# S5 mixer: part of u scaled through a diagonal, first two gelus alone, six tiles of the gated GEMM in split parts

## The chip, the cores and the metric

The program runs on one core of one Trainium2 chip. The metric is the device time of one execution in microseconds, as the median of several runs. TensorE (PE), its weight loads (PEld), VectorE (DVE), ScalarE (ACT), GpSimd (POOL) and the DMA queue of SyncE (SP) each run their own list of instructions in the order written and wait for one another by semaphores. TensorE's clock has two levels, 1.2 and 2.4 GHz; the profile shows the granted one as a share of 2.4 GHz.

## The reference

Two layers over x of 256 rows (sequence) by 2048 columns, in float32. Layer 0 is a differential attention, layer 1 the S5 mixer; each is followed by a squared-relu MLP, with an rmsnorm ahead of each of the four and at the end. The change touches the S5 mixer alone:

```python
h = rmsnorm(x, norm_mix[1])                 # x * rstd(row) * gain
u = h.reshape(B, S, 128 groups, 16)
bu = B_bar u ; x_t = a x_(t-1) + bu_t       # complex diagonal state, per group
y = Re(C x) + d_skip * h
g = gelu(y)
val, gate = split(g @ w_glu, 2)             # w_glu is 2048 x 4096
x = x + val * sigmoid(gate)
```

## The kernel before

x stays in SBUF as two row tiles `xres[0]`, `xres[1]` of 128 x 2048. Weights come from HBM in chunks of two 128-row k-tiles by 512 columns (512 KB, tag `raw`, 5 buffers). `prep` (L181) cuts a chunk into two fp32r parts: ACT writes the high part `wh` (L191) and DVE the rest `wl` (`sub`, L113), four buffers each. Every GEMM outside the S5 phase takes three matmuls per product, high by high, high by low, low by high (`ktile`, L199, lines L201 to L203), from a left side that is split in the same way.

The S5 phase (`s5_phase`, L1092) handles the 2048 columns as 16 tiles of 128. For tile j:

- `s5_u` (L999) transposes x of two tiles on TensorE into one PSUM bank (L1004), and ACT copies the bank out in 16 pieces (L1009) in another order. The tiles 0 to 7 are done before the phase; the tiles 8 to 15 in the loop, at the end of the steps 1, 3, 5 and 7.
- `s5_scale` (L1013) multiplies u of two tiles by rstd in the permuted order (`rsb`). `rsb` comes from a small matmul into the bank `prs` (L1100) and a copy (L1102). The first pair is scaled on DVE, the others on POOL.
- `s5_e` (L1019): 32 matmuls into an `sd` bank (L1026), then on DVE two products, add, subtract, two scans, two products and a subtract, and one add on POOL (L1047). The result X[j] is the state that enters `s5_y`.
- `s5_y` (L1050): 48 matmuls (L1061) into a `y` bank that two tiles share. After the second tile ACT does gelu in 16 pieces (L1068), then casts g to the high part `blk.h` of the left side for the later GEMMs (L1072), and POOL subtracts to get the low part `blk.l` (L1073).
- `glu_tile` (L1079): the first 512 value and 512 gate columns of the GEMM, four float32 matmuls of 512 columns (L1085) from g and the raw weight chunk, without a split. It runs three steps behind (`LAG`).

The order in the loop is written out by hand. Step j issues `s5_e(j+1)`, the scale of tile j+4, `glu_tile(j-3)`, `s5_y(j)`, `s5_u(j+7)` at odd j, and the table fetch of tile j+4 on SP (`s5_fetch`, L978: three DMAs of 512 KB). After the loop the three last `glu_tile` follow. There are eight PSUM banks: four accumulators, two `sd` banks in turn (4 and 5), two `y` banks in turn (6 and 7). `s5_u` takes an `sd` bank too:

```python
rings["sd"], rings["y"] = [4, 5], [6, 7]
groups = [(0, 1), (2, 3), (4, 5), (6, 7), (8, 9), (10, 11), (12, 13), (14,), (15,)]
```

`keep_warm` (L320) issues matmuls whose results nobody reads: 18, 4 and 12 of them (`WARM`) while the head of the phase waits. After the phase `evict_val` (L1262) and `evict_gate` (L1270) empty the accumulators, and the next GEMMs take `glu_lhs`.

Of the kernel before, what the change touches and what calls it, by code (L numbers as in the profile page):

```python
# [16 lines left out]
P = 128  # L17
# [5 lines left out]
KB = 4  # L23
# [15 lines left out]
Q = 4  # L39

SLOTS_HOP = 3
WARM = (18, 4, 12)
LAG = 3


class Lhs:
# [11 lines left out]
def tile_trunk(  # L58
# [39 lines left out]
    def bank():  # L98
        return ring("sd")

    def tmp(shape, tag, bufs=None, dt=F32):
        if bufs is None:
            return sb.tile(shape, dt, tag=tag, name=nm(tag))
        return sb.tile(shape, dt, tag=tag, name=nm(tag), bufs=bufs)
# [10 lines left out]
    def tsc(o, a, s1, op0, s2=None, op1=None):  # L115
        if op1 is None:
            v.tensor_scalar(out=o, in0=a, scalar1=s1, scalar2=None, op0=op0)
        else:
            v.tensor_scalar(out=o, in0=a, scalar1=s1, scalar2=s2, op0=op0, op1=op1)
# [21 lines left out]
    def until(cond):  # L141
        while not cond():
            assert side
            pump()
# [32 lines left out]
    def load_next():  # L177

        load(len(raws))

    def prep(i):  # L181
        if i >= len(stream) or i in preps or GLU0 <= i < GLU0 + 16:
            return
        r = raws[i]
        h = wp.tile([P, WK, BW], F32R, tag="wh", name=nm("wh"), bufs=LIVE)
        l = wp.tile([P, WK, BW], F32R, tag="wl", name=nm("wl"), bufs=LIVE)
        preps[i] = (h, l)
        step = 1 if i < FINE else WK
        for k in range(0, WK, step):
            sl = slice(k, k + step)  # L190
            act.copy(h[:, sl], r[:, sl])  # L191
            if FINE <= i < POOL:
                sub(l[:, 0], r[:, 0], h[:, 0].bitcast(F32))
                pool_e.tensor_tensor(out=l[:, 1], in0=r[:, 1], in1=h[:, 1].bitcast(F32), op=ALU.subtract)
            else:
                sub(l[:, sl], r[:, sl], h[:, sl].bitcast(F32))
        load_next()

    def ktile(accs, lhs, k, wh, wl, t, first, last):  # L199
        ts = slice(t * P, (t + 1) * P)  # L200
        pe.matmul(accs[t], lhs.h[:, k, ts], wh, start=first, stop=False)  # L201
        pe.matmul(accs[t], lhs.h[:, k, ts], wl, start=False, stop=False)  # L202
        pe.matmul(accs[t], lhs.l[:, k, ts], wh, start=False, stop=last)  # L203
# [20 lines left out]
    def new_accs():  # L224
        return [ring("acc") for _ in range(NT)]
# [94 lines left out]
    def keep_warm(n):  # L320

        if n == 0:
            return
        a = ring("acc")
        for _ in range(n):
            pe.matmul(a, x1[3].h[:, 0, 0:P], x1[3].h[:, 0:2], start=True, stop=True)
# [669 lines left out]
        pool_e.memset(dk[:, :, 0:1], 0.0)  # L996
        return dk

    def s5_u(j):  # L999

        ps = bank().rearrange("p (i s) -> p i s", s=S)
        for i in range(2):
            for t in range(NT):
                pe.transpose(ps[:, i, t * P:(t + 1) * P], xres[t][:, (j + i) * P:(j + i + 1) * P], ident)  # L1004
        u = tmp([P, 2, Q, NCH], "vsb", bufs=4)
        pv = ps.rearrange("p i (k s) -> p i s k", s=L)
        for s in range(L):
            for q in range(Q):
                act.copy(u[32 * s:32 * s + 32, :, q], pv[32 * q:32 * q + 32, :, L - 1 - s])  # L1009
            yield s  # L1010
        U[j] = u

    def s5_scale(j, rsb, eng=pool_e):  # L1013
        u = U[j]
        uv = u.rearrange("p i q k -> p (i q) k")
        eng.tensor_tensor(out=uv, in0=uv, in1=rsb[:, None, :].broadcast_to([P, 2 * Q, NCH]), op=ALU.mult)
        U[j], U[j + 1] = u[:, 0], u[:, 1]

    def s5_e(j):  # L1019
        te, to, tt, ct = tab[j]  # L1020
        u, dk = U[j], DK.pop(j)
        pe_ = bank().rearrange("p (i q k) -> p i q k", i=2, q=Q)
        for i in range(2):
            for q in range(Q):
                for h in (slice(0, GP), slice(GP, P)):
                    pe.matmul(pe_[h, i, q], te[:, i, q, h], u[:, q], start=True, stop=True)  # L1026
        sh = [P, 2, Q, NCH]
        tw = tmp([P, 2] + sh[1:], "c5")
        t1, t2 = tw[:, 0], tw[:, 1]
        mult(t1, pe_, ct[:, 0:1].broadcast_to(sh))  # L1030
        mult(t2, pe_, ct[:, 1:2].broadcast_to(sh))
        add(t1[:, 0], t1[:, 0], t2[:, 1])
        sub(t1[:, 1], t1[:, 1], t2[:, 0])
        zz = tmp(sh, "s2k", bufs=7)
        for i in range(2):
            v.tensor_tensor_scan(out=zz[:, i].rearrange("p q k -> p (q k)"), data0=dk.rearrange("p q k -> p (q k)"),
                                 data1=t1[:, i].rearrange("p q k -> p (q k)"), initial=0.0,
                                 op0=ALU.mult, op1=ALU.add)
        n = NCH - 1
        shn = [P, 2, Q, n]  # L1040
        w1, w2 = tmp(sh, "s2k", bufs=7), tmp(sh, "s2k", bufs=7)
        mult(w1[:, :, :, 0:n], zz[:, :, :, 0:n], ct[:, 0:1, :, 0:n].broadcast_to(shn))
        mult(w2[:, :, :, 0:n], zz[:, :, :, 0:n], ct[:, 1:2, :, 0:n].broadcast_to(shn))
        xp = tmp(sh, "bc", bufs=4)
        pool_e.memset(xp[:, :, :, 0:1], 0.0)
        sub(xp[:, 0, :, 1:], w1[:, 0, :, 0:n], w2[:, 1, :, 0:n])
        pool_e.tensor_tensor(out=xp[:, 1, :, 1:], in0=w1[:, 1, :, 0:n], in1=w2[:, 0, :, 0:n], op=ALU.add)  # L1047
        X[j] = xp

    def s5_y(grp):  # L1050
# [25 lines left out]
        for jj, j in enumerate(grp):  # L1076
            G[j] = g[:, jj]

    def glu_tile(j):  # L1079

        g = G.pop(j)
        c, kk = GLU0 + j // WK * 2, j % WK
        for i, accs in ((c, a_v), (c + 1, a_g)):
            for t in range(NT):
                pe.matmul(accs[t], g[:, t * P:(t + 1) * P], raws[i][:, kk], start=j == 0, stop=j == NJ - 1)  # L1085
            if j == NJ - 1 and i == c:
                first_vals.extend(evict_val(a_v))
            if kk == WK - 1:
                load_next()
                pos[0] += 1  # L1090

    def s5_phase(norm):  # L1092
        until(lambda: norm.done)
        keep_warm(WARM[0])
        ar = tmp([P, NT, P], "s1k", bufs=4)
        for t in range(NT):
            tsc(ar[:, t], sela.rearrange("p s r -> p (s r)"), norm.rstd[:, t:t + 1], ALU.mult)
        prs = bank()[:, 0:NCH]
        for t in range(NT):
            pe.matmul(prs, ar[:, t], selb[:, t], start=(t == 0), stop=(t == NT - 1))  # L1100
        rsb = tmp([P, NCH], "rsb", bufs=1)
        v.tensor_copy(rsb, prs)  # L1102
        keep_warm(WARM[1])
        s5_scale(0, rsb, v)
        for j in range(3):
            DK[j] = s5_dk(j)
        s5_scale(2, rsb)
        s5_e(0)
        keep_warm(WARM[2])
        groups = [(0, 1), (2, 3), (4, 5), (6, 7), (8, 9), (10, 11), (12, 13), (14,), (15,)]  # L1110
        ys = {}
        for grp in groups:
            gen = s5_y(grp)
            for j in grp:
                ys[j] = (gen, j == grp[-1])
        for j in range(NJ):
            if j + 1 < NJ:
                s5_e(j + 1)
            if j + 3 < NJ:
                DK[j + 3] = s5_dk(j + 3)  # L1120
            if j % 2 == 0 and j + 4 < NJ and j + 4 in U:
                s5_scale(j + 4, rsb)
            if j >= LAG:
                glu_tile(j - LAG)
            gen, end = ys[j]
            next(gen)
            if end:
                for _ in gen:
                    pass
            if j % 2 == 1 and j + 7 < NJ:  # L1130
                for _ in s5_u(j + 7):
                    pass
            s5_fetch(j + 4)
            pump()
        for j in range(NJ - LAG, NJ):
            prep(GLU0 + 16 + j - NJ + LAG)
            glu_tile(j)


    x0 = [Lhs() for _ in range(NB)]  # L1140
# [121 lines left out]
    def evict_val(accs):  # L1262
        vs = []
        for t in range(NT):
            n = tmp([P, BW], "vsb", bufs=4)
            act.copy(n, accs[t])
            vs.append(n)
        return vs

    def evict_gate(accs, vs, u):  # L1270
        for t in range(NT):
            sg = tmp([P, BW], "s2k", bufs=7)
            act.activation(sg, accs[t], AF.Sigmoid)  # L1273
            mult(vs[t], vs[t], sg)
            xs = xres[t][:, u * BW:(u + 1) * BW]
            add(xs, xs, vs[t])
        spawn(xT_block(x3[u], u, 2, norm3, "a"), 2)

    a_v, a_g = new_accs(), new_accs()
    s5_phase(norm2)  # L1280
    evict_gate(a_g, first_vals, 0)
    for u in range(1, NB):
        a = gemm(glu_lhs)
        vs = evict_val(a)
# [60 lines left out]
```

## Time and profile before

| | |
|---|---|
| median of 3 runs | 2136.08 us (2135.87 to 2137.46) |
| profiled execution | 2133.82 us, its span 2132.0 us |
| PE busy | 2082.6 us (98%) |
| PEld, DVE, ACT, POOL busy | 1765.5, 1365.7, 1050.6, 164.6 us |
| granted clock, mean | 0.992 |
| S5 phase in the span | about 1130 to 1281 us |

The busy shares are means over the whole program. TensorE sets the time nearly everywhere; in the slices of the span one place stands out, where PE falls to 7 tenths, PEld to 4 and the clock below 9: the S5 phase. All times below are microseconds from the start of the span.

### The profile page before, as it was taken

To read this page: it belongs to the slowest core of one execution; us is meant where nothing else is said; L and a number is where in the kernel's file an instruction comes from. 1 tells how busy PE (TensorE), PEld (TensorE's weight loads), DVE (VectorE), ACT (ScalarE), POOL (GpSimd) and SP (SyncE) were. 2 spreads that over 40 slices of the span, in tenths; PEclk is the share of its full clock that TensorE was granted. 3 is DMA by queue.
4 is the path that set the end of the run, shared out by engine and by line. 5 is a ranking of instruction groups with operands and counts; after the bars stand their busy time and mean duration, and the time that the engine had idled before them with its cause. 6 is when DMAs were issued, how large, how long until landed. Compare 5 with 4: busy or idle time off the path is not lost. (4 is left out here: it accounts for less than half of the span.)

```text
span 2132.0 us, 31756 instructions
## 1 busy us (share of the span) xinstructions
PE 2082.6 (98%) x12098; PEld 1765.5 (83%) x12098; DVE 1365.7 (64%) x2284; ACT 1050.6 (49%) x1598; POOL 164.6 (8%) x282
## 2 busy tenths in 40 slices
PE   8999999999999999999997799999999999999998
PEld 8899988888888888888885457888888888888886
DVE  5775656788588667767766465556555645655655
ACT  5445545555445545544483565545434434434443
POOL 2000200021021002101102220000000000000000
PEclk9999999999999999999999899999999999999999
DMA  7467755687676867876785656565556556555553
GB/s 247 157 198 233 248 179 173 222 246 268 230 235 212 295 215 224 281 237 222 238 288 206 234 181 205 181 217 176 203 193 189 189 193 193 174 207 188 193 192 129
DMA packets 230813, 452.57 MB, mean 212 GB/s; under 512 B 20818, under 2 KB 29348, under 8 KB 230660
## 3 DMA queue, kind: packets, MB, share of 16 engines
q1 hardware_dynamic: 218400, 416.34, 58.9%
q0 software_dynamic: 11440, 32.86, 4.8%
q8 instruction: 95, 1.56, 0.3%
q10 hardware_dynamic: 820, 1.34, 0.2%
q14 instruction: 58, 0.48, 0.1%
HBM read 420.85 MB, written 41.68 MB: 217 GB/s over the span
## 5 line engine op out<-in xcount | busy, mean ns | idle before, releaser
L113 DVE TENSOR_TENSOR wl<-raw,wh 128x1024 fp32r<-128x1024 f32 (+1 forms) x690 | 833.5, 1218 | 581.7 <-ACT wh L191 577.7
L191 ACT CAST wh<-raw 128x1024 fp32r<-128x1024 f32 (+1 forms) x690 | 713.0, 1047 | 633.1 <-PE acc L203 344.9
L201 PE MATMUL acc<-wh,x 128*128 128x512 f32 x832 | 326.5, 392 | 2.4 <-ACT s2k L1273 2.4
L203 PE MATMUL acc<-wh,x 128*128 128x512 f32 x832 | 324.0, 389 | 0.0
L202 PE MATMUL acc<-wl,x 128*128 128x512 f32 x832 | 323.9, 389 | 0.0
L265 PE MATMUL acc<-x,wh 128*128 128x512 f32 x1024 | 273.9, 394 | 2.8 <-DVE s2k L110 2.8
L265 PE MATMUL acc<-a,wh 128*128 128x512 f32 x1024 | 272.7, 393 | 0.0
L201 PE MATMUL acc<-wh,a 128*128 128x512 f32 x640 | 251.6, 393 | 0.0
L202 PE MATMUL acc<-wl,a 128*128 128x512 f32 x640 | 249.4, 390 | 0.1
L203 PE MATMUL acc<-wh,a 128*128 128x512 f32 x640 | 249.3, 390 | 0.0
L265 PEld LDWEIGHTS acc<-x,wh 128*128 128x128 f32 x1024 | 177.2, 189 | 29.0 <-DVE s2k L110 3.2
L265 PEld LDWEIGHTS acc<-a,wh 128*128 128x128 f32 x1024 | 177.4, 189 | 25.0
L201 PEld LDWEIGHTS acc<-wh,x 128*128 128x128 f32 x832 | 156.2, 188 | 34.8 <-ACT s2k L1273 3.3
L203 PEld LDWEIGHTS acc<-wh,x 128*128 128x128 f32 x832 | 156.2, 188 | 32.9
L202 PEld LDWEIGHTS acc<-wl,x 128*128 128x128 f32 x832 | 156.3, 188 | 31.9
L269 PEld LDWEIGHTS acc<-a,wl 128*128 128x128 f32 x1024 | 152.8, 190 | 18.7
L269 PEld LDWEIGHTS acc<-x,wl 128*128 128x128 f32 x1024 | 152.4, 190 | 18.8
L269 PE MATMUL acc<-x,wl 128*128 128x256 f32 x1024 | 158.0, 282 | 0.0
L269 PE MATMUL acc<-a,wl 128*128 128x256 f32 x1024 | 157.5, 281 | 0.0
L248 PE MATMUL acc<-x,wh 128*128 128x256 f32 x512 | 148.5, 290 | 1.2 <-ACT wh L191 1.2
L250 PE MATMUL acc<-x,wl 128*128 128x256 f32 x512 | 145.7, 284 | 0.0
L249 PE MATMUL acc<-x,wh 128*128 128x256 f32 x512 | 145.5, 284 | 0.0
(238 smaller groups left out, 2140.8 us busy)
## 6 DMA issues: line engine op xcount, KB each, us to landing
raw<-in_mlp_w_dram SPq DMA_DIRECT2D x512, 512.0 KB
raw<-in_a_w_in_dram SPq DMA_DIRECT2D x94, 512.0 KB
raw<-in_b_w_glu_dram SPq DMA_DIRECT2D x64, 512.0 KB
raw<-in_a_w_out_dram SPq DMA_DIRECT2D x32, 512.0 KB
scr<-t POOLq DMA_DIRECT2D x32, 512.0 KB, 5.4
teo<-scr SPq DMA_DIRECT2D x32, 512.0 KB
t<-scr SPq DMA_DIRECT2D x16, 512.0 KB
pwr<-pwn SPq DMA_DIRECT2D x16, 256.0 KB
```

What stands on the lines that cost most here:

```text
L113: v.tensor_tensor(out=o, in0=a, in1=b, op=ALU.subtract)
L191: act.copy(h[:, sl], r[:, sl])
L201: pe.matmul(accs[t], lhs.h[:, k, ts], wh, start=first, stop=False)
L202: pe.matmul(accs[t], lhs.h[:, k, ts], wl, start=False, stop=False)
L203: pe.matmul(accs[t], lhs.l[:, k, ts], wh, start=False, stop=last)
L248: pe.matmul(o, wh[:, kk, cs], lhs.h[:, k], start=f and c % 2 == 0, stop=False)
L249: pe.matmul(o, wh[:, kk, cs], lhs.l[:, k], start=False, stop=False)
L250: pe.matmul(o, wl[:, kk, cs], lhs.h[:, k], start=False, stop=e and c % 2 == 1)
L265: pe.matmul(a[c], wh, lhs.hl[:, k].rearrange("p i s -> p (i s)"), start=first, stop=False)
L269: pe.matmul(a[c][:, S:], wl, lhs.h[:, k], start=False, stop=last)
```

## The change

- `s5_u` can take a diagonal matrix `diag` (rstd of the row on its diagonal) in place of the identity. The transposes of tiles 8 to 15 become ordinary float32 matmuls of x by `diag`, and their u comes out scaled: the POOL multiplications for the pairs 8, 10, 12 and 14 go. ACT makes `diag` in two activations.
- u of the tiles 8 to 11 is done before the loop, after `s5_e(0)`; u of 12 and 13 at the end of step 2, of 14 and 15 at the end of step 4. The third `keep_warm` has 4 matmuls in place of 12. The new u tiles lie in other buffers (one `wh` buffer, the tags `ct` and `junk`).
- The first pair is scaled by DVE straight from the bank `prs`; the copy `rsb` comes after.
- One gelu on a single element is issued at the head of the phase.
- The tiles 0 and 1 have gelus of their own. `glu_tile(0)` moves to step 2, `glu_tile(1)` to step 3, step 4 has none, and from step 5 on the lag is three as before.
- For the tiles 8 to 13 the weight chunks go through `prep`, two at each of the steps 9, 11 and 13, and `glu_tile` takes `ktile` with `blk.h` and `blk.l`: twelve fp32r matmuls in place of four float32 ones. `prep` issues the next weight load itself.

```diff
-WARM = (18, 4, 12)
+WARM = (18, 4, 4)
 LAG = 3
+WHOLE = 8
     def prep(i):
-        if i >= len(stream) or i in preps or GLU0 <= i < GLU0 + 16:
+        if i >= len(stream) or i in preps or GLU0 <= i < GLU0 + 16 and not WHOLE <= (i - GLU0) // 2 * WK < NJ - 2:
             return
-    def s5_u(j):
+    def s5_u(j, u=None, diag=None):
...
-                pe.transpose(ps[:, i, t * P:(t + 1) * P], xres[t][:, (j + i) * P:(j + i + 1) * P], ident)
-        u = tmp([P, 2, Q, NCH], "vsb", bufs=4)
+                o, xs = ps[:, i, t * P:(t + 1) * P], xres[t][:, (j + i) * P:(j + i + 1) * P]
+                if diag is None:
+                    pe.transpose(o, xs, ident)
+                else:
+                    pe.matmul(o, xs, diag[:, t], start=True, stop=True)
...
     def glu_tile(j):
...
-        for i, accs in ((c, a_v), (c + 1, a_g)):
+        for i, accs in ((c, A["v"]), (c + 1, A["g"])):
             for t in range(NT):
-                pe.matmul(accs[t], g[:, t * P:(t + 1) * P], raws[i][:, kk], start=j == 0, stop=j == NJ - 1)
+                if i in preps:
+                    wh, wl = preps[i]
+                    ktile(accs, blk, j % KB, wh[:, kk], wl[:, kk], t, j == 0, j == NJ - 1)
+                else:
+                    pe.matmul(accs[t], g[:, t * P:(t + 1) * P], raws[i][:, kk], start=j == 0, stop=j == NJ - 1)
...
             if kk == WK - 1:
-                load_next()
+                if i in preps:
+                    del preps[i]
+                else:
+                    load_next()
                 pos[0] += 1
     def s5_phase(norm):
         until(lambda: norm.done)
+        act.activation(warm_act, warm_act, AF.Gelu_apprx_tanh)
         keep_warm(WARM[0])
         ar = tmp([P, NT, P], "s1k", bufs=4)
+        diag = wp.tile([P, NT, P], F32, tag="wl", name="diag", bufs=LIVE)
         for t in range(NT):
             tsc(ar[:, t], sela.rearrange("p s r -> p (s r)"), norm.rstd[:, t:t + 1], ALU.mult)
+            act.activation(diag[:, t], ident, AF.Copy, scale=norm.rstd[:, t:t + 1])
...
+        keep_warm(WARM[1])
+        s5_scale(0, prs, v)
         v.tensor_copy(rsb, prs)
-        keep_warm(WARM[1])
-        s5_scale(0, rsb, v)
...
         s5_e(0)
+        u8 = wp.tile([P, 2, 2, Q, NCH], F32, tag="wh", name="u8", bufs=LIVE)
+        for i in range(2):
+            for _ in s5_u(8 + 2 * i, u8[:, i], diag):
+                pass
         keep_warm(WARM[2])
+        A["v"], A["g"] = new_accs(), new_accs()
-        groups = [(0, 1), (2, 3), (4, 5), (6, 7), (8, 9), (10, 11), (12, 13), (14,), (15,)]
+        groups = [(0,), (1,), (2, 3), (4, 5), (6, 7), (8, 9), (10, 11), (12, 13), (14,), (15,)]
...
-            if j % 2 == 0 and j + 4 < NJ and j + 4 in U:
+            if j in (0, 2):
                 s5_scale(j + 4, rsb)
-            if j >= LAG:
-                glu_tile(j - LAG)
+            if j % 2 == 1 and WHOLE <= j - 1 and j + 1 <= NJ - 2:
+                for i in range(2):
+                    prep(GLU0 + j - 1 + i)
+            if j in (2, 3) or j >= 2 + LAG:
+                glu_tile(glu)
+                glu += 1
...
-            if j % 2 == 1 and j + 7 < NJ:
-                for _ in s5_u(j + 7):
+            if j in (2, 4):
+                u = tmp([P, 2, Q, NCH], "ct" if j == 2 else "junk", bufs=1)
+                for _ in s5_u(12 if j == 2 else 14, u, diag):
                     pass
```

## Rows read from the trace of the kernel before

**Rows 1.** Waits of PE, 1125 to 1285: us in total, times, longest.

```profile
PE sd L1026 <- ACT vsb L1009: 21.4, 4, 7.0
PE y L1061 <- issue: 5.2, 3, 2.2
...
PE acc L1085 <- ACT s2k L1068: 0.6, 1, 0.6
```

**Rows 2.** Timeline around the second stall: start, duration, engine, line; idle before in brackets.

```profile
1171.00 6.58 ACT L1068 ACTIVATE s2k<-y 32x128 f32<-32x128 f32 x16 [8.37 <-PE y L1061]
...
1177.61 0.62 ACT L1072 CAST x<-s2k 128x512 fp32r<-128x512 f32 x1
...
1178.26 4.28 ACT L1009 COPY vsb<-sd 32x128 f32<-32x128 f32 x16
...
1182.59 1.97 PE L1026 MATMUL sd<-vsb,teo 128*64 128x64 f32 x32 [4.79 <-ACT vsb L1009]
```

**Rows 3.** Chain that ended last: the last stall's step, and an unstalled step.

```profile
1223.18 1.97 PE sd L1026 x32
1225.15 5.22 PE acc L1085 x8
1230.37 1.55 PE y L1061 x48
1231.92 0.93 PE sd L1026 x32
1232.85 3.63 PE acc L1085 x8
```

**Rows 4.** Windows: stretch, length, busy PE, PEld, DVE, ACT, POOL; clock, DMA, GB/s.

```profile
1150.00:1160.00 10.00, 3.31 (x84) 2.75 (x82) 8.45 (x16) 9.69 (x25) 3.16 (x8) 1.00 0.64 218
1160.00:1170.00 10.00, 7.32 (x62) 4.39 (x64) 4.93 (x9) 2.52 (x10) 2.81 (x6) 0.66 0.00 0
...
1181.00:1184.00 3.00, 1.41 (x26) 1.41 (x28) 0.00 (x0) 1.48 (x6) 1.06 (x2) 0.50 0.96 389
```

**Rows 5.** Timeline of the phase's head.

```profile
1134.90 0.66 PE L1100 MATMUL sd<-selb,s1k 128*128 128x64 f32 x4
...
1135.60 0.23 DVE L1102 COPY rsb<-sd 128x64 f32<-128x64 f32 x1 [0.56 <-PE sd L1100]
1135.86 0.69 DVE L1016 TENSOR_TENSOR vsb<-vsb,rsb 128x512 f32<-128x512 f32 x1
...
1137.80 1.29 DVE L107 TENSOR_TENSOR c<-sd,t 128x512 f32<-128x512 f32 x2 [1.25 <-PE sd L1026]
...
1149.88 1.28 ACT L1068 ACT_TABLE_LOAD   x1 [17.40 <-PE y L1061]
```

**Rows 6.** Timeline of the phase's end.

```profile
1263.70 4.64 ACT L1068 ACTIVATE s2k<-y 32x64 f32<-32x64 f32 x16
...
1268.26 10.57 PE L1085 MATMUL acc<-raw,s2k 128*128 128x512 f32 x24
...
1281.25 0.50 PE L201 MATMUL acc<-wh,x 128*128 128x512 f32 x1 [2.42 <-ACT s2k L1273]
```

**Rows 7.** Timeline of TensorE in a GEMM with split parts, before the phase.

```profile
1107.82 0.39 PE L202 MATMUL acc<-wl,a 128*128 128x512 f32 x1
...
1108.05 0.39 PE L203 MATMUL acc<-wh,a 128*128 128x512 f32 x1
```

**Rows 8.** The page's costliest groups: busy, mean ns of one, idle before.

```profile
L113 DVE TENSOR_TENSOR wl<-raw,wh 128x1024 fp32r<-128x1024 f32 (+1 forms) x690 | 833.5, 1218 | 581.7 <-ACT wh L191 577.7
L191 ACT CAST wh<-raw 128x1024 fp32r<-128x1024 f32 (+1 forms) x690 | 713.0, 1047 | 633.1 <-PE acc L203 344.9
```

**Rows 9.** Timeline: the four transposes of one u, and POOL's low part of a pair.

```profile
1170.88 0.66 PE L1004 MATMUL sd<-ident,xres 128*128 128x128 f32 x4
...
1178.31 1.26 POOL L1073 TENSOR_TENSOR x<-s2k,x 128x512 fp32r<-128x512 f32 x1 [7.48 <-ACT x L1072]
```

**Rows 10.** Windows, columns as in rows 4: a stretch with many transfers.

```profile
1193.00:1196.00 3.00, 3.00 (x8) 1.18 (x7) 2.97 (x6) 2.92 (x8) 0.00 (x0) 1.00 0.98 396
```

More of the change, by code (lines that the diff above doesn't have):

```diff
@@ L1003, in s5_u @@
             for t in range(NT):
-                pe.transpose(ps[:, i, t * P:(t + 1) * P], xres[t][:, (j + i) * P:(j + i + 1) * P], ident)
-        u = tmp([P, 2, Q, NCH], "vsb", bufs=4)
+                o, xs = ps[:, i, t * P:(t + 1) * P], xres[t][:, (j + i) * P:(j + i + 1) * P]
[3 more added lines that the diff above has]
+                    pe.matmul(o, xs, diag[:, t], start=True, stop=True)
+        if u is None:
+            u = tmp([P, 2, Q, NCH], "vsb", bufs=4)
         pv = ps.rearrange("p i (k s) -> p i s k", s=L)
@@ L1010, in s5_u, with s5_scale @@
             yield s
-        U[j] = u
-    def s5_scale(j, rsb, eng=pool_e):
+        if diag is None:
+            U[j] = u
+        else:
+            U[j], U[j + 1] = u[:, 0], u[:, 1]
+    def s5_scale(j, factor, eng=pool_e):
         u = U[j]
         uv = u.rearrange("p i q k -> p (i q) k")
-        eng.tensor_tensor(out=uv, in0=uv, in1=rsb[:, None, :].broadcast_to([P, 2 * Q, NCH]), op=ALU.mult)
+        eng.tensor_tensor(out=uv, in0=uv, in1=factor[:, None, :].broadcast_to([P, 2 * Q, NCH]), op=ALU.mult)
         U[j], U[j + 1] = u[:, 0], u[:, 1]
@@ L1077, in s5_y @@
             G[j] = g[:, jj]
+    A = {}
     def glu_tile(j):
-        g = G.pop(j)
+        g, blk = G.pop(j), glu_lhs[j // KB]
         c, kk = GLU0 + j // WK * 2, j % WK
-        for i, accs in ((c, a_v), (c + 1, a_g)):
+        for i, accs in ((c, A["v"]), (c + 1, A["g"])):
             for t in range(NT):
-                pe.matmul(accs[t], g[:, t * P:(t + 1) * P], raws[i][:, kk], start=j == 0, stop=j == NJ - 1)
+                if i in preps:
[3 more added lines that the diff above has]
+                    pe.matmul(accs[t], g[:, t * P:(t + 1) * P], raws[i][:, kk], start=j == 0, stop=j == NJ - 1)
             if j == NJ - 1 and i == c:
-                first_vals.extend(evict_val(a_v))
+                first_vals.extend(evict_val(accs))
             if kk == WK - 1:
-                load_next()
+                if i in preps:
+                    del preps[i]
+                else:
+                    load_next()
                 pos[0] += 1
@@ L1115, in s5_phase @@
                 ys[j] = (gen, j == grp[-1])
+        glu = 0
         for j in range(NJ):
@@ L1134, in s5_phase @@
             pump()
-        for j in range(NJ - LAG, NJ):
-            prep(GLU0 + 16 + j - NJ + LAG)
-            glu_tile(j)
+        while glu < NJ:
+            prep(GLU0 + 16 + glu - NJ + LAG)
+            glu_tile(glu)
+            glu += 1
     x0 = [Lhs() for _ in range(NB)]
@@ L1277, in evict_gate @@
         spawn(xT_block(x3[u], u, 2, norm3, "a"), 2)
-    a_v, a_g = new_accs(), new_accs()
     s5_phase(norm2)
-    evict_gate(a_g, first_vals, 0)
+    evict_gate(A["g"], first_vals, 0)
     for u in range(1, NB):
```

## The prediction

> **What bounds the kernel now.** Over the whole program TensorE does, so I looked for the places where it waits. The waits of PE come first [rows 1]: in the S5 phase it sat idle 21.4 us in four waits for ACT's copies of u, and 5.2 us in three waits at the head. The timeline shows why [rows 2]. The transposed u of a pair lies in one of the two `sd` banks until ACT has copied it out. ACT takes things in order: 16 gelus of the pair before (6.58 us), a cast (0.62), then the 16 copies (4.28). `s5_e` of the step after next needs that bank, so TensorE stood still for 4.79 us and DVE had nothing to do. The windows show a second price [rows 4]: after such a wait the granted clock is 0.50, the 1.2 GHz level. The chain gives it in time [rows 3]: in the step after the last stall `s5_e` took 1.97 us and the gated product 5.22; in a step without stall 0.93 and 3.63. That is 2.63 us lost; the four stalls lost 2.16, 2.4, 2.6 and 2.6 in this way, by the same reading. Stalls and slow clock together cost about 31 us. A step without a stall is 0.93 + 3.63 + 1.55 = 6.11 us of TensorE [rows 3], while DVE's chain of one tile is 4.93 (one tile lies in the second row of [rows 4]). TensorE bounds such a step, and DVE the head.
>
> **The change, part by part.** I lay out the new phase in the time of the profiled span and compare the start of the next GEMM's first matmul, 1281.25 [rows 6].
>
> *Head.* The copy to `rsb` (0.23 us) leaves the path of the first scale [rows 5]: `s5_e(0)` and DVE's first product start some 0.25 earlier, at 1137.55. The gelu table load of 1.28 [rows 5] moves to a time when ACT is idle, after 1132. `diag` is two ACT operations on 128 columns behind rstd (ready when DVE starts on `ar`, 1134.6); under 1 us, done before the first u is asked for. Eight float32 products by `diag` take the place of transposes. The trace has four transposes of 128 columns at 0.15 each to the next matmul (0.66 for the four with the end) [rows 9] and two float32 matmuls of 64 columns in 0.66 with their end [rows 5], which would be 0.66 for one of 128 if all of it grew with the columns. Bounds: 0.15 and 0.66 each; I take 0.25, as streaming 128 columns at a quarter of the 0.86 us of a 512 column float32 product (10.57 us for 12) gives 0.22 [rows 6]. So 1.0 us for a u of four.
>
> The Trainium skill (TensorE: Matmul & The Clock Gate, section Terms) says that the transpose mode is four times faster for float32 than an ordinary matmul, which speaks against this edit. By that rule a u would take 4 x 0.59 = 2.4 us, and the two that stand in the chain below (the first, and that of tile 12) would add 2.8 us.
>
> The 32 copies of u8 to u11 (8.56 us, twice the 4.28 of [rows 2]) run on ACT from 1138.4 to 1147.0. They hold both `sd` banks, so `s5_e(1)` waits until 1142.7 and `s5_e(2)` until 1147.0. This costs little, since DVE is the bound there: one without a wait would begin tile 1 at 1142.5 and tile 2 at 1147.4 (4.93 each), and with the held banks it begins them at 1143.9 and 1148.9. The eight `keep_warm` matmuls that go stood in this wait.
>
> *First gelus.* gelu(0) of 16 pieces of 64 columns takes 4.64 [rows 6]: 1147.0 to 1151.7. From there a chain, each link with its duration from the rows named: glu(0) 3.63 to 1155.35; y(2) 1.55 to 1156.9 (X(2) is there by 1155.3); u12 1.0; e(4) 0.93 to 1158.85 (its bank is free, u12 has the other); glu(1) to 1162.5; y(3) to 1164.05; gelu(2,3) 6.6 to 1170.7. ACT has copied u12 by 1162.2. TensorE, which has no glu in step 4, does e(5), y(4), u14 and e(6) by 1168.4 and waits 2.3 us for that gelu: this is what stands in place of the old stall. A wait of 2.2 at the head [rows 1] left the clock at 1.00 [rows 4], so I charge no slow clock. glu(2) ends at 1174.4, y(5) at 1175.95. u14 is copied from 1171.3 to 1175.6, just in time for e(7).
>
> *Middle.* Steps 6 to 9 are four TensorE steps of 6.11: y(9) ends at 1200.4. gelu(4,5) is done 0.4 us before glu(4) asks. POOL loses four scalings and one add stays behind its subtract; DVE has 1.2 us spare in each step. Both hidden.
>
> *Split tiles.* A split product is three matmuls at 0.227 [rows 7], a glu tile 12 x 0.227 + 0.2 = 2.92 in place of 3.63 (the 0.2 is what a float32 tile takes over its four products). Six tiles would give 4.3 us. But the loop gives little of it, because glu now needs more behind the gelu: the cast (0.62) and, from the third matmul on, POOL's low part, 1.26 [rows 9]. The cycle of a pair is then y to gelu 6.6, cast 0.65, low part 1.3, the other ten matmuls 2.45, y 1.55: 12.55 us, above the 12.22 of two float32 steps. For the three pairs: y(11) at 1213.05 (12.65, as e, a float32 glu(7), y and e bring TensorE to glu(8) about when the cast ends). For tiles 10 and 11, five `wh` buffers are wanted where four are: the copy of chunk 11 waits for u8, which y(11) reads last. ACT stands there, queued behind it gelu(10,11), which waits for y(11) too; so the copy of 1.05 comes on top [rows 8]: y(13) at 1226.7 (13.65). The last pair: y(15) at 1239.25 (12.55). DVE's six `sub` are 1.22 each [rows 8]; e(13) starts on DVE at 1215.4, 2.5 late, and X(13) comes at 1220.5, before y(13) at 1225. Hidden; its cover is the wait for gelu. If ACT and POOL were faster, DVE would be next, at 2 x 4.93 + 2.44 = 12.3 a pair.
>
> *Tail.* glu(13) split 2.92, glu(14) and glu(15) 6.86 (eight products at 0.857): TensorE is done at 1249.05, where it was 1278.55. The next GEMM waits for the evictions and the sigmoid's table. Before, ACT came late to them by a wait for a weight chunk; now the chunks come earlier in the order. I take its start at 1251.0, 30.3 us earlier.
>
> *DMA.* Weight loads of steps 9 to 13 come a step earlier than before and stand ahead of a fetch on SP; two of them wait for `sub` of chunks 8 and 9. From 1188 to 1207 about 10.5 MB is issued. At 396 GB/s [rows 10] this is 26 us, done at 1214; the last of it, the fetch of tile 14, is wanted at 1218. No stall, with 4 us to spare.
>
> *Sum.* 2133.82 - 30.3 = 2103.5 for the profiled execution. The median lies 2.26 above that execution: 2105.8. I add 1.2 us for some ten hand-overs between engines at about 0.1 that the chain leaves out: **2107**, own range 2102 to 2112.
>
> **Rivals.**
> - *The split pays in full.* If the cast and low part were there in time, the three pairs would take one float32 and five split steps, 33.1 in place of 38.85 us: 2101. For it: ACT is free before each gelu. Against: before the change one glu already waited 0.6 us for its gelu [rows 1], as a float32 product with no cast to wait for.
> - *The transfers become late.* Over 10 us the queues moved 218 GB/s in the first window of [rows 4]. Midway between that and [rows 10], at 307, the 10.5 MB end at 1222, 4 us after the fetch of tile 14 is wanted, and tile 15 waits as much again: 2115. Against: in that window little was asked for (DMA share 0.64).
> - *The stalls come back.* The two u in the loop, 12 and 14, still pass ACT behind gelus. If each costs a stall of 4.8 and a slow step of 2.6, the time is 2107 + 15 = 2122. Against: step 4 has no glu, and the bank is asked for later.
> - *The other side: the clock stays low.* With 8 `keep_warm` matmuls fewer, TensorE works some half of the time from 1141 to 1151. If it went to 1.2 GHz there and the waits of about 2 us at each pair kept it there, a step would cost up to 6.1 more. After five such steps the gain is gone; over ten the time is 2107 + 61, 2168. Against: the head before was as thin (3.31 of 10 us busy at clock 1.00) [rows 4], and the clock fell only in waits of 4.8 us or more. The change would then not do what it says.
> - *Dear products.* At the upper bound of 0.66 each, the two u in the chain add 2 x 1.6: 2110. The rule quoted above would come to the same. Against: 128 columns in the long float32 products stream in 0.22.
>
> **How the numbers follow.** Chances: forecast 0.65, dear products 0.05, split in full 0.08, late transfers 0.12, stalls back 0.06, low clock 0.04. The range takes in the first four cases: 2100 to 2116. A measurement of this kernel tells 0.2%, 4.3 us, from no change. All cases but the last are faster than that: faster 0.95, same 0.01, slower 0.04.
>
> **What would show it.** Right: no wait of PE `sd` for ACT copies over 2.3 us, clock 1.00 from 1140 on; copies of u from 1138 to 1147 with e(1), e(2) behind them; one wait of about 2.3 before glu(2); y(9) near 1200; waits of glu(10) and glu(12) for the cast and POOL; next GEMM at 1251. Wrong: a clock of 0.50 anywhere in the phase, e(13) or e(14) waiting for a fetch, or glu tiles 8 to 13 at 2.9 us with no wait ahead of them.

## The result, and the profile after

The change takes the median from 2136.36 us (2135.87 to 2137.46, 4 runs) to 2108.22 us (2106.14 to 2108.93, 4 runs): a ratio of 0.9866, 95% interval 0.9849 to 0.9883, 28.1 us less. The forecast was 2107. The profiled execution took 2108.14 us with a span of 2106.4; the mean granted clock rose from 0.992 to 0.997. Lines in the new file are a little lower: L1009 became L1015 (copies of u), L1026 L1035 (`s5_e`), L1061 L1070 (`s5_y`), L1068 L1077 (gelu), L1072 L1081 (cast), L1073 L1082 (low part), L1085 L1101 (float32 gated product); `ktile` is L202 to L204, the products by `diag` are L1009.

First the waits of TensorE, 1125 to 1270 us, in the kernel after (us in total, times, longest):

```profile
PE acc L202 <- ACT x L1081: 3.9, 3, 1.9
PE sd L1035 <- ACT u L1015: 3.7, 2, 1.9
PE acc L204 <- POOL bc L1054: 2.5, 3, 1.0
PE acc L1101 <- ACT s2k L1077: 1.5, 1, 1.5
PE sd L446 <- DVE xres L111: 1.0, 1, 1.0
PE y L1070 <- issue: 0.8, 1, 0.8
```

The 21.4 us behind the copies [rows 1] are gone. What is left of them, 3.7 in two waits, stands in the head. Behind the first DVE waits 1.57 us in its turn; behind the second it has work without a gap, so that one costs DVE nothing. New are 6.4 us before the split tiles (cast and low part), 1.5 for one gelu, and 1.0 after the phase. (The trace names POOL's memset L1054 for the low part: it stands right behind it on POOL.)

The timeline of ACT in the head, kernel after (start, duration, engine, line; idle before in brackets):

```profile
1133.25 1.28 ACT L1113 ACT_TABLE_LOAD   x1
...
1134.66 0.39 ACT L1119 ACTIVATE diag<-ident,nrstd 128x128 f32<-128x128 f32 x1
...
1139.50 8.57 ACT L1015 COPY u<-sd 32x128 f32<-32x128 f32 x32 [3.67 <-PE sd L1009]
1148.10 4.66 ACT L1077 ACTIVATE s2k<-y 32x64 f32<-32x64 f32 x16
```

and that of TensorE beside it:

```profile
1138.30 1.16 PE L1009 MATMUL sd<-diag,xres 128*128 128x128 f32 x8
...
1143.83 1.15 PE L1035 MATMUL sd<-vsb,teo 128*64 128x64 f32 x32 [1.92 <-ACT u L1015]
...
1148.12 1.15 PE L1035 MATMUL sd<-vsb,teo 128*64 128x64 f32 x32 [1.75 <-ACT u L1015]
...
1150.16 1.02 PE L1070 MATMUL y<-bc,teo 128*64 128x64 f32 x8 [0.77 <-issue]
...
1152.89 1.43 PE L1035 MATMUL sd<-vsb,teo 128*64 128x64 f32 x32
```

The copies of u8 to u11 are one block in front of the first gelu, and `s5_e(1)` and `s5_e(2)` stand behind its halves. The last line takes 1.43 where the same work takes 1.15 above: the clock has fallen. The windows say when (stretch, length, busy PE, PEld, DVE, ACT, POOL; clock, DMA share, GB/s):

```profile
1148.00:1150.00 2.00, 1.27 (x36) 1.13 (x36) 1.93 (x5) 1.91 (x8) 0.31 (x1) 1.00 0.78 240
...
1151.00:1153.00 2.00, 2.00 (x43) 2.00 (x40) 1.97 (x4) 1.90 (x8) 1.33 (x2) 0.50 0.70 258
...
1180.00:1190.00 10.00, 10.00 (x112) 5.51 (x113) 8.79 (x15) 6.26 (x16) 3.40 (x9) 1.00 0.95 349
...
1210.00:1220.00 10.00, 8.94 (x118) 6.92 (x113) 9.83 (x15) 5.39 (x11) 5.17 (x8) 1.00 1.03 379
1220.00:1230.00 10.00, 7.45 (x139) 5.98 (x140) 9.86 (x16) 6.14 (x13) 3.23 (x7) 1.00 0.90 336
1230.00:1240.00 10.00, 7.29 (x106) 5.78 (x102) 9.86 (x14) 9.30 (x26) 2.45 (x3) 0.95 0.33 107
```

From 1180 to 1210 TensorE is busy all the time at full clock: here the change does all that was hoped. From 1210 to 1240, the split tiles, it idles again, and now DVE is busy 9.83 to 9.86 of 10 us. The second pair of split tiles in the timeline of TensorE:

```profile
1224.43 0.50 PE L202 MATMUL acc<-wh,x 128*128 128x512 f32 x1 [1.58 <-ACT x L1081]
...
1226.14 0.50 PE L204 MATMUL acc<-wh,x 128*128 128x512 f32 x1 [0.97 <-POOL bc L1054]
```

and what ACT did for it, with the prep of a chunk held by the last reader of u8 ahead of the gelu:

```profile
1216.11 1.05 ACT L192 CAST wh<-raw 128x1024 fp32r<-128x1024 f32 x1 [4.49 <-PE y L1070]
1217.18 6.55 ACT L1077 ACTIVATE s2k<-y 32x128 f32<-32x128 f32 x16
1223.76 0.62 ACT L1081 CAST x<-s2k 128x512 fp32r<-128x512 f32 x1
```

The phase's end, TensorE again:

```profile
1247.52 7.03 PE L1101 MATMUL acc<-raw,s2k 128*128 128x512 f32 x16
1253.98 0.79 PE L202 MATMUL acc<-wh,x 128*128 128x512 f32 x1
...
1258.51 0.55 PE L446 MATMUL sd<-ident,xres 128*128 128x128 f32 x3 [1.00 <-DVE xres L111]
```

The next GEMM starts at 1253.98 without the wait of 2.42 of [rows 6], 27.3 us earlier than 1281.25. This execution reached the phase (DVE's first operation on `ar`) 0.75 us later than that of before, 1135.31 against 1134.57, so within the phase it is 28.0. In the profiles used here the phase starts anywhere from 1133.99 to 1139.80, with the same code up to there, so times within it are best counted from its start.

### The profile page after: what moved, and what is told of

It is laid out like the page before. It is cut to its first block, busy times and chain, and to the rows that moved or that the text cites. A ratio compares the mean times of both kernels' runs of the same rounds, so it can differ in the third digit from the quotient of the medians.

```text
span 2106.4 us, 31862 instructions
## 1 busy us (share of the span) xinstructions
PE 2073.0 (98%) x12130; PEld 1767.3 (84%) x12130; DVE 1380.2 (66%) x2290; ACT 1059.7 (50%) x1624; POOL 163.3 (8%) x279
## 4 chain that ended last, share of the span: by engine, by line
PE 92%; ACT 3%; DVE 2%; DMA 1%; issue 1%; POOL 0%; SPq 0%; ACTq 0%
PE acc L266 22%; PE acc L204 16%; PE acc L202 16%; PE acc L203 16%; PE acc L270 11%; PE acc L249 2%; PE acc L251 2%; PE acc L250 2%; ACT s2k L1077 1%; PE acc L1101 1%; ACT wh L192 1%; PE y L1070 1%; DVE wl L114 1%; DMA raw<-in_a_w_in_dram 1%; DMA raw<-in_mlp_w_dram 1%
## 5 line engine op out<-in xcount | busy, mean ns | idle before, releaser
L114 DVE TENSOR_TENSOR wl<-raw,wh 128x1024 fp32r<-128x1024 f32 (+1 forms) x696 | 842.6, 1220 | 580.2 <-ACT wh L192 579.4
L202 PE MATMUL acc<-wh,x 128*128 128x512 f32 x856 | 337.4, 394 | 3.9 <-ACT x L1081 3.9
L204 PE MATMUL acc<-wh,x 128*128 128x512 f32 x856 | 334.5, 391 | 2.5 <-POOL bc L1054 2.5
L203 PE MATMUL acc<-wl,x 128*128 128x512 f32 x856 | 333.8, 390 | 0.0
L202 PE MATMUL acc<-wh,a 128*128 128x512 f32 x640 | 251.6, 393 | 0.0
L204 PE MATMUL acc<-wh,a 128*128 128x512 f32 x640 | 249.3, 390 | 0.0
L202 PEld LDWEIGHTS acc<-wh,x 128*128 128x128 f32 x856 | 161.2, 188 | 37.5 <-ACT x L1081 4.3
L204 PEld LDWEIGHTS acc<-wh,x 128*128 128x128 f32 x856 | 161.0, 188 | 37.4 <-POOL bc L1054 3.8
L203 PEld LDWEIGHTS acc<-wl,x 128*128 128x128 f32 x856 | 161.1, 188 | 32.9 <-DVE wl L114 0.2
```

The source lines that it names most:

```text
L114: v.tensor_tensor(out=o, in0=a, in1=b, op=ALU.subtract)
```

## The experiments

Each was timed beside the kernel before on the same chip: 2135.92 us (2131.94 to 2137.53, 15 runs) for the first four, 2134.7 (2132.38 to 2135.5, 7 runs) for the next four, 2133.27 (2132.0 to 2138.28, 7 runs) for the four at the end, which are there to compare on one chip. My theory at that point: the new place of u gives the whole gain, the split costs time, and a short fall of the clock takes 3 us of the gain. The rivals: the split or the smaller edits carry part of the gain.

**No split.** All 16 tiles as float32 products.

```diff
-WHOLE = 8
+WHOLE = 16
```

Expected: 

> The changed kernel with all 16 gated tiles as float32 products (no weight parts for tiles 8 to 13). Theory: in the loop the split tiles wait for the cast and for POOL's low part, so splitting costs there. In the changed kernel y(9) to y(15) takes 41.4 us (three pairs of 12.7, 14.2 and 14.4); three float32 pairs take 36.7; the tail loses 0.7. So this kernel is about 4 us faster: 2104, with no wait of TensorE for the cast or the low part and no fall of the clock near the end. Rival: the split pays its 4.3 us, and leaving it out gives 2112.5.

Measured: 2104.16 (2102.26 to 2104.96), ratio 0.9853 (0.984 to 0.9867). Some 4 us below the whole change, if two chips may be compared; the run side by side is below. From the phase's start to the next GEMM it took 113.6 us against 118.7. The lead of 5 us shrinks behind the phase, where the transposes of the next GEMM wait twice for the residual:

```profile
1248.57 0.54 PE L202 MATMUL acc<-wh,x 128*128 128x512 f32 x1
...
1252.43 0.33 PE L446 MATMUL sd<-ident,xres 128*128 128x128 f32 x1 [0.81 <-DVE xres L111]
1253.75 0.90 PE L446 MATMUL sd<-ident,xres 128*128 128x128 f32 x3 [1.00 <-DVE xres L111]
```

The 0.90 for three transposes, 0.55 after the whole change, is the clock at its lower level again.

**The u edit alone.** The kernel before with the new u, and nothing else but `new_accs` behind `keep_warm`: gelus in pairs, table load late, `rsb` path, 12 `keep_warm`, lag 3, no split. Against the whole change:

```diff
-WARM = (18, 4, 4)
+WARM = (18, 4, 12)
-WHOLE = 8
+WHOLE = 16
-        act.activation(warm_act, warm_act, AF.Gelu_apprx_tanh)
-        s5_scale(0, prs, v)
+        s5_scale(0, rsb, v)
-        groups = [(0,), (1,), (2, 3), ...
+        groups = [(0, 1), (2, 3), ...
-            if j in (2, 3) or j >= 2 + LAG:
+            if j >= LAG:
```

Expected: 

> The kernel before with the u edit alone: u of tiles 8 to 15 through the diagonal, 8 to 11 ahead of the loop, 12 and 14 in steps 2 and 4; pairs of gelus, late gelu table, the first scale through rsb, 12 warm matmuls, lag 3 and no split as before. Theory: the u edit removes the four stalls with their slow clock and is nearly the whole gain: 2103 to 2107, about the same as the kernel without split. Rival: the single gelus and the early table carry a good part; then 2112 to 2120.

Measured: 2104.59 (2103.89 to 2110.19), 0.9862 (0.9848 to 0.9877). One part alone gives all that the whole change gives. Beside the kernel without split on the same chip, 2104.16, the single gelus, the early table and the direct scale together are worth nothing that can be told from no change. The profiled execution, the longest of the four, is an exception: at 1157.33 `s5_y` has waited 2.92 for the state of tile 2, whose last subtract on DVE ends at 1157.23, with no gated product to fill the time; the clock is 0.83 from 1150 to 1170; and glu(2) starts 40.8 us after the phase's start, 37.3 without the split. The other three runs, 5.2 to 6.3 us shorter, do not bear that out.

**The old u in the new kernel.** u of the tiles 8 to 15 transposed in the loop as before, scaled on POOL; 12 `keep_warm`; the rest as after.

```diff
-            if j in (2, 4):
...
+            if j % 2 == 1 and j + 7 < NJ:
+                for _ in s5_u(j + 7):
```

Expected: 

> The changed kernel with u of tiles 8 to 15 made as before (transposes at steps 1, 3, 5, 7, POOL scaling, 12 warm matmuls), all else as changed. Theory: the four waits of s5_e for ACT's copies come back, each about 4.8 us and followed by a clock of 0.50: 2130 to 2140, no clear gain over the kernel before. Rival: the other edits carry the gain; then 2112 or less.

Measured: 2133.85 (2131.06 to 2138.33, 11 runs), 0.9994 (0.9985 to 1.0003). No difference from the kernel before. The waits of TensorE, 1125 to 1270:

```profile
PE sd L1035 <- ACT vsb L1015: 20.5, 4, 8.5
...
```

and two of its steps in the timeline:

```profile
1181.57 1.98 PE L1035 MATMUL sd<-vsb,teo 128*64 128x64 f32 x32 [8.54 <-ACT vsb L1015]
...
1202.22 1.98 PE L1035 MATMUL sd<-vsb,teo 128*64 128x64 f32 x32 [4.80 <-ACT vsb L1015]
```

With u in its old place the four stalls are back, with 1.98 at the lower clock behind them as in [rows 2]. This and the run before show from both sides that the stalls are what the change removes. The new u is two things at once, another place and a product that scales on the way; no run takes them apart.

**Twelve keep_warm.** The fall of the clock at 1151 tested by itself.

```diff
-WARM = (18, 4, 4)
+WARM = (18, 4, 12)
```

Expected: 

> The changed kernel with 12 in place of 4 warm matmuls after the first u. They end at about 1143.5 in its profile, where s5_e(1) starts at 1143.8 by its wait for the copies, so they delay nothing. Theory: the clock, which fell to 0.50 from 1150.2 to 1153.5 in the changed kernel, stays up, worth 1.5 us: 2106.5. Rival: the clock falls all the same, because the waits of TensorE between 1146 and 1150 are untouched: 2108.

Measured: 2105.93 (2105.73 to 2106.41), 0.9863 (0.9848 to 0.9878), 2.3 us below the median of the change on another chip; the ratios overlap, so by time alone the step is not certain. The windows show it:

```profile
1150.00:1160.00 10.00, 9.87 (x169) 7.21 (x169) 9.76 (x15) 8.32 (x30) 5.16 (x10) 1.00 0.77 266
...
1230.00:1240.00 10.00, 7.59 (x68) 5.56 (x67) 8.88 (x12) 9.64 (x29) 3.37 (x4) 0.83 0.32 105
```

The clock is 1.00 where the change had 0.83 over 1150 to 1160, and glu(2) starts 37.3 us after the phase's start, 38.3 in the change: the early fall costs 1.0. That the 12 matmuls keep the clock up is not shown by this. The kernel with a lag of four, below, has 4 of them and the same instructions as the change up to there, and its clock stayed at 1.00 all the same, with glu(2) 37.3 after the phase's start:

```profile
1150.00:1160.00 10.00, 9.24 (x145) 6.54 (x147) 9.79 (x16) 8.31 (x30) 6.12 (x11) 1.00 0.71 245
```

The fall at the last split pair is still there with 12, behind waits of 1.93 and 0.48 us; nothing was done about that one.

**A lag of four for the split tiles**, so that cast and low part are long done when the tile comes.

```diff
-            if j in (2, 3) or j >= 2 + LAG:
+            if j in (2, 3) or j >= 2 + LAG and j != 11:
```

Expected: 

> The changed kernel with the glu tiles 8 to 15 one step later (no glu in step 11, four tiles after the loop). The waits of TensorE for the cast (3.9 us) and for POOL's low part (2.5 us) must go. Theory: DVE is the next bound, because in the changed kernel it was busy 9.8 to 9.9 of every 10 us from 1200 to 1240 and a pair of tiles with two weight parts takes it 12.9 us or more, above the 12.2 of a float32 pair on TensorE; the gain is then only what two more split tiles give after the loop, 1.4 us, and the clock: 2104 to 2106, and TensorE waits in its place for the state (POOL's add or DVE). Rival: the gelu chain alone held the split back; then the six tiles give 4.3 us over the kernel without split: 2100.

Measured: 2108.13 (2107.57 to 2109.4), 0.9876 (0.986 to 0.9893). No gain: the waits for cast and low part vanish, and the same time is lost elsewhere. Its waits:

```profile
PE y L1070 <- issue: 8.1, 5, 3.0
PE sd L1035 <- ACT u L1015: 3.7, 2, 1.9
PE sd L1035 <- DMA teo<-scr: 1.6, 1, 1.6
```

`s5_y` now waits for its state. "issue" names no releaser; DVE's timeline does. One pair of tiles in this kernel, from one pair of `sub` to the next:

```profile
1203.25 3.07 DVE L114 TENSOR_TENSOR wl<-raw,wh 128x1024 fp32r<-128x1024 f32 x2
1206.25 1.28 DVE L108 TENSOR_TENSOR c<-sd,t 128x512 f32<-128x512 f32 x2
...
1209.54 2.35 DVE L108 TENSOR_TENSOR s2k<-s2k,t 128x504 f32<-128x504 f32 x2
...
1217.21 3.10 DVE L114 TENSOR_TENSOR wl<-raw,wh 128x1024 fp32r<-128x1024 f32 x2
```

1217.21 - 1203.25 = 13.96 us a pair without a gap, above the 12.22 that TensorE wants for two float32 steps. So even with no wait on ACT or POOL a split pair is slower than a pair without the split. The theory named the right next bound and its size too small; the rival of 2100 falls.

**A lag of four, and `sub` of the split chunks on POOL**, to take those 3.1 us off DVE.

```diff
-                sub(l[:, sl], r[:, sl], h[:, sl].bitcast(F32))
+                (pool_e if GLU0 <= i < GLU0 + 16 else v).tensor_tensor(
+                    out=l[:, sl], in0=r[:, sl], in1=h[:, sl].bitcast(F32), op=ALU.subtract)
```

Expected: 

> As the kernel with the later glu tiles, and the low parts of the twelve weight chunks' subtraction on POOL in place of DVE. Theory (DVE bounds the loop once the gelu chain doesn't): DVE falls to 9.9 us a pair, TensorE bounds with 10.8, and the split pays: 2100 to 2102. Rival: POOL's subtract, about 2.5 us for a chunk by its 1.26 for half of that, stands ahead of its add for the state and of the low part of g, and slows DVE when both read SBUF; then 2106 or more.

Measured: 2113.29 (2111.34 to 2116.45), 0.9903 (0.9888 to 0.9917), 5 us slower than the lag alone; the theory was wrong and its rival right. POOL in this kernel, and DVE beside it:

```profile
1203.48 4.86 POOL L197 TENSOR_TENSOR wl<-raw,wh 128x1024 fp32r<-128x1024 f32 x2
```

```profile
1203.96 2.15 DVE L111 TENSOR_TENSOR c<-c 128x256 f32<-128x256 f32 x1
1206.03 2.59 DVE L114 TENSOR_TENSOR c<-c 128x256 f32<-128x256 f32 x1
1208.55 2.34 DVE L1046 TENSOR_TENSOR_SCAN s2k<-s1k,c 128x256 f32<-128x256 f32 x2
```

Two chunks take 4.9 us on POOL against some 3.1 on DVE. DVE, which was to be relieved, takes 2.15, 2.59 and 2.34 meanwhile for an add, a subtract and two scans that take 0.43, 0.42 and 1.27 ten microseconds later, while POOL is idle: 5.0 us more, for the 3.1 that were moved. POOL's add for the state is not what is late; it has itself waited 1.89 for DVE when it starts at 1212.28. The waits of `s5_y` grow to 10.5 us in five, the longest 3.9. How much of the 5 us is the clock is not taken apart: it was at the lower level for 17 us of the phase, for 3.4 with the lag alone.

**The accumulators taken before `keep_warm`**, as in the kernel before.

```diff
         keep_warm(WARM[0])
+        A["v"], A["g"] = new_accs(), new_accs()
...
         keep_warm(WARM[2])
-        A["v"], A["g"] = new_accs(), new_accs()
```

Expected: 

> The changed kernel with the accumulators of the gated GEMM taken ahead of the warm matmuls, as in the kernel before. Theory: the next GEMM then takes the gate's banks again, as before, and its first matmul waits about 2.4 us for the sigmoid, where in the changed kernel it followed the last glu product at once; the wait of 1.0 us for the residual in the transposes goes in exchange: 2109 to 2110. Rival: the wait only moves and the time stays 2108.

Measured: 2108.88 (2107.13 to 2110.63), 0.9881 (0.9866 to 0.9895). The time does not tell the two theories apart. The trace shows what moves: a wait of 1.7 us of the next GEMM's first product for the sigmoid is back, and the wait of 1.0 for the residual is gone:

```profile
PE acc L202 <- ACT s2k L1307: 1.7, 1, 1.7
```

**The best of these together**: no split, 12 `keep_warm`, and the transposes of the first block behind the phase spawned with 6 in place of 2, to lie further back among the next GEMM's products.

```diff
-        spawn(xT_block(x3[u], u, 2, norm3, "a"), 2)
+        spawn(xT_block(x3[u], u, 2, norm3, "a"), 6 if u == 0 else 2)
```

Expected: 

> No split, 12 warm matmuls, and the transposes for the next norm block four steps later after the first gate. Theory: the parts that cost go: 2104.2 for no split, 1.5 less for the clock in the head, 1.8 to 3 less for the waits for the residual and the clock behind them after the phase: 2100 to 2101. Rival: the waits at the end are covered later by slack of the norm, and nothing is gained beyond 2103.

Measured: 2100.85 (2099.93 to 2102.03), 0.9843 (0.9829 to 0.9858), below both kernels. All its waits of TensorE over 1125 to 1270:

```profile
PE y L1070 <- issue: 1.8, 2, 1.0
PE sd L1035 <- ACT u L1015: 1.7, 1, 1.7
PE acc L1101 <- ACT s2k L1077: 1.2, 2, 0.6
PE sd L1009 <- DVE c L108: 0.4, 1, 0.4
PE y L1070 <- POOL bc L1056: 0.4, 2, 0.2
```

None is left behind the phase.

**Four kernels on one chip**, to see what the chips had to do with the differences, and which part of the last version does its work. The whole change again:

Expected: 

> The whole change once more, beside the runs without the split on the same chip. Theory (the split costs some 4 us): 2107 to 2109, and 3.5 to 5 us above the run without the split. Rival (the 4 us between the earlier runs came from the chips): within 2 us of it.

No split, 4 `keep_warm`:

Expected: 

> No split, 4 keep_warm matmuls, on the same chip as the whole change. Theory: 2103 to 2105. Rival: 2106 to 2108, as the whole change.

No split, 12 `keep_warm`:

```diff
-WARM = (18, 4, 4)
+WARM = (18, 4, 12)
-WHOLE = 8
+WHOLE = 16
```

Expected: 

> No split and 12 keep_warm matmuls in the third place. Theory (a fall of the clock near 1150 costs 1.5 us or more): 2102 to 2103, 1.5 to 2 us below the run with 4, clock 1.00 from 1140 to 1160. Rival (the clock's fall lies where TensorE would wait anyway): the same time as with 4, 2104.

The same with the transposes spawned with 6:

Expected: 

> As the run with no split and 12 keep_warm, with the first block's transposes spawned with 6 in place of 2. Theory (the wait for the residual, 1.8 us behind the phase, and the slow clock behind it cost 1.5 to 2 us): 2100.5 to 2101.5. Rival (keep_warm gave all of the 3.3 us): no difference from the run without the 6.

Measured, in this order:

| | median us (range, 4 runs each) | ratio to before (95%) |
|---|---|---|
| whole change | 2108.6 (2107.62 to 2112.26) | 0.9875 (0.9856 to 0.9894) |
| no split | 2103.94 (2101.92 to 2106.92) | 0.9856 (0.9838 to 0.9874) |
| no split, 12 `keep_warm` | 2103.74 (2102.45 to 2104.15) | 0.9853 (0.9837 to 0.9869) |
| and later transposes | 2101.16 (2099.48 to 2101.48) | 0.984 (0.9824 to 0.9856) |

The whole change takes 4.7 us longer than the kernel without the split; the two ranges do not touch. Not all of that is the split: its profile has the early fall of the clock again, ahead of the first split tile, and glu(2) 38.1 us after the phase's start. Where the profile has no such fall, with 12 `keep_warm` on the chip of the first four, the split costs 1.8 (2105.73 to 2106.41 with it, 2102.26 to 2104.96 without it and with 4). So it costs in every comparison, between 1.8 and 4.7 us. My theory of `keep_warm` fell: without the split the 12 matmuls give nothing, and the forecast of 2100 to 2101 for the version above was met with a term in it, 1.5 for the clock, that is worth nothing. With 4 of them the clock falls there too, 0.83 over 1140 to 1150, but some 5 us earlier in the phase than in the whole change, ahead of the second wait for ACT's copies of u, which takes up the loss. `s5_e(2)` with 4 and with 12:

```profile
1146.82 1.24 PE L1035 MATMUL sd<-vsb,teo 128*64 128x64 f32 x32 [0.67 <-ACT u L1015]
```

```profile
1147.15 1.15 PE L1035 MATMUL sd<-vsb,teo 128*64 128x64 f32 x32 [1.76 <-ACT u L1015]
```

glu(2) starts 37.3 us after the phase's start in both. The transposes give the 2.6 us, 1.6 of them the two waits for the residual, and the clock behind those waits. The stretch behind the phase, with the transposes early:

```profile
1250.00:1260.00 10.00, 8.35 (x34) 6.42 (x33) 6.98 (x10) 6.07 (x13) 0.00 (x0) 0.83 0.80 250
```

and late:

```profile
1250.00:1260.00 10.00, 10.00 (x49) 8.28 (x49) 7.13 (x10) 6.32 (x10) 0.00 (x0) 1.00 0.90 288
```

## Why the prediction was right, and where it was not

The main mechanism is shown: removing the stalls and the slow steps behind them gives the time, and the edit of u alone does it. Term by term, the forecast shifted by 0.75 us for the later start of the phase:

- *Head.* The early table load lies in idle ACT time as forecast. The copies took 8.57 (8.56 forecast) and ended at 1148.07, where 1147.75 was forecast.
- *Products by `diag`.* Four start 1.09 us before the next matmul: 0.27 each, 0.25 forecast. The Trainium skill (TensorE: Matmul & The Clock Gate, section Terms) gives the transpose mode a factor of four for float32; the trace shows 1.09 to 0.59, a factor of 1.85. The rival of dear products falls.
- *First gelus.* Forecast: glu(2) at 1171.5 behind a wait of 2.3. Measured: 1173.59 behind a wait of 1.52, 2.1 late. The step that failed is "so I charge no slow clock". It rested on waits of 2.2 us in the head of the kernel before that left the clock at 1.00, and on "the clock fell only in waits of 4.8 us or more". Here waits of 1.92, 1.75 and 0.77, with work between them, left it at 0.50. In the kernel with a lag of four waits of 1.91, 1.74 and 0.77 left it at 1.00, so the length of the waits alone is not what decides. This fall cost 1.0 (38.3 against 37.3 from the phase's start). The other 1.1 is in the chain without a fall too: hand-overs, and links a little longer than I took them (e(4) is 1.08 to the next product, 0.93 forecast), for which 1.2 was added.
- *Middle.* Steps of 6.11 as forecast; y(9) at 1203.35, 2.2 late by what came before.
- *Split pairs.* Forecast 12.65, 13.65, 12.55; measured 12.97, 13.96, 14.47 from one end of `s5_y` to the next. The chain is the one forecast: gelu, cast, low part, ten products. What was short: the low part took 1.62 and 1.43 in the last two pairs in place of 1.26, and in the last pair the clock fell again, seven gaps of 0.42 to 0.59 between products in place of 0.227: from the low part's first product to `s5_y` 3.98 us, 2.50 in the pair before, so 1.5 for the clock. DVE as next bound was mis-sized: 12.3 forecast, 13.96 with the lag of four. Its two `sub` take 3.07 there (2.44 assumed), and a product pair 2.35 in place of 1.28 where it meets POOL's low part.
- *End.* Forecast: next GEMM 1.95 us behind the last glu. Measured: none. I had not seen that `new_accs` behind `keep_warm` changes which banks come next: the next GEMM gets the value banks, emptied first, and not one that waits for the sigmoid; the run with the accumulators taken early has that wait again. That is 2 us better than forecast, and 1.0 of it goes in the new wait for the residual.
- *DMA.* 379 and 336 GB/s from 1210 to 1230 and no wait of TensorE for a transfer: as forecast. With the lag of four one of 1.6 us appears, so the margin was small.
- *Sum.* The next GEMM starts 28.0 us earlier within the phase, 30.3 forecast: clock 2.5 (1.0 early, 1.5 late), hand-overs and longer links 1.1, low parts and small change of the pairs 1.1 worse; banks 1.95 and the last three glus 0.46 better. From the phase's start to the end of the span the gain is 26.3, so 1.7 more is given back behind the phase, of which the wait for the residual is 1.0 and the rest is not traced. For the profiled execution I forecast 2103.5 and it took 2108.14. The forecast of 2107 came within 1.2 of the median because I added 1.2 for hand-overs, and 2.26 because the profiled execution of before lay that far below its median; that of after lies on its median. The size is right in part by offsetting errors; the mechanism is right by the runs with and without the u edit.

Of the rivals, "the split pays in full" is wrong in sign: the split costs 1.8 to 4.7 us. "The clock stays low" came true twice, for 3.4 us each time, and not for good: it was back at 1.00 by 1153.8 and by 1242.4, with TensorE at work without a gap since 1150.8 and 1239.1. The prediction had named a clock of 0.50 anywhere in the phase as a sign of being wrong; the sign appeared, at a price of 2.5 us and not of the gain.

## What to carry to other kernels

When an engine that works in order empties a bank between two long jobs, move the emptying to a time when the bank's next user is not the bound; here that, with the scaling taken into the product, gave 31 us. Before an operation is cut into cheaper parts, add up what every helper engine must do per step, with durations measured while its neighbours run: a saving of 0.7 us a tile on TensorE cost DVE 1.5 us a tile and lost 1.8 to 4.7 us in the whole. When a phase gets shorter, look at the work that follows it: here 2.6 us lay in two transposes that now came too early.

## What was not expected of the hardware

- The clock falls in one execution and not in another behind the same work and the same waits. In the kernels with 4 `keep_warm`, whose code is the same up to there but for the place of the accumulators in one, it fell 14.9 and 14.5 us after the phase's start in the two profiled executions of the whole change, 9.6 us after it in both without the split, 9.8 with the accumulators taken early, 8.9 with the `sub` on POOL, and not at all with the lag of four. None of the four profiles of the other kernels with the whole change's head and 12 shows a fall there; with the u edit alone, which has 12 too, it fell at 20.1. So neither the length of the waits nor the number of `keep_warm` matmuls is shown to decide it; what does is open.
- DVE and POOL slow each other: DVE's two products of 128x504 take 1.28 us alone and 2.36 while POOL's low part runs (1210.30 to 1212.66 after the change, the low part from 1210.76 to 1212.12), and the low part took 1.36 to 1.62 there, 1.26 in [rows 9].
- A 128x1024 subtract takes 2.45 us on POOL (4.9 for two) and 1.22 as a mean on DVE ([rows 8]), 1.54 in this phase (3.07 for two), so the move from DVE to POOL costs POOL 1.6 to 2 times what it saves, and slows DVE besides.
- The table load cost 1.28 us early or late. At the head of the phase it lay in idle time of ACT; together with the two other small edits that moved the median by nothing that could be told.
